# Down-projection weight pairs in the ring of the up projection's weight tiles

## The chip, the cores and the metric

One core of one Trainium2 chip. The metric is the device time of one execution in microseconds; the number told is the median of several runs of the same program. The kernel is written with a tile framework: the program names tiles out of pools ("rings" of a fixed number of buffers under one tag), and a scheduler sets the order of the instructions on each engine when the program is built, then adds the waits. An engine takes its instructions in that order. A tile can be written only when the last user of the buffer that it gets is done.

## The reference

A decoder of two layers on one sequence of 1024 tokens, model width 1024. Each layer:

```
h   = x @ W_in                     # columns split among four mixers
y_A = multi-head latent attention  # causal softmax, rotary keys
y_B = Mamba-2 SSD                  # causal convolution on x/B/C, chunked scan
y_C = multi-scale retention        # rotary q/k, chunkwise recurrence
y_D = RG-LRU branch                # causal convolution, gates, linear recurrence
x   = LayerNorm(alpha * x + concat(y_A, y_B, y_C, y_D) @ W_out)
x   = LayerNorm(alpha * x + SwiGLU(x))   # hidden width 2816
```

## The kernel before

All matrix products run on TensorE in tiles of 128 x 128 weights against 512 columns. Each float32 operand is split into a rounded part and a remainder, and a product is three matmuls: high by high, high by low, low by high. The rounded part is a copy on ScalarE (`A`, ACT), the remainder a subtraction on VectorE (`V`, DVE; L127 is the line of the helper `tt`, so most of the two-operand operations of DVE and of GpSimd, `G`, POOL, stand under L127).

The feed-forward part uses a seven-product scheme of Strassen's kind for 2 x 2 blocks, in both of its projections. In the up projection the hidden width is cut into NF = 22 tiles f. Tiles 0 and 1 are done plainly (`f_plain`), while `x_sums` makes the sums of the input blocks on VectorE and GpSimd. Then `f_block(f)` runs for f = 2 to 21. It loads two rows of weights (`g`, `u`, tiles named `raw`, 512 KB each), casts and splits `g` (`gw`) and half of `u` (`uw`), makes four sums in place on GpSimd (L127, raw<-raw), splits the two results (`s12`, `s34`; with `gw` the tiles named `ws`), and runs seven products of 12 matmuls, 84 in all. The hidden halves go to DRAM (`ha_d`), with sums of them by `to_h`: for each pair of tiles GpSimd makes one difference `s3` and three more, deferred in `later`.

The down projection needs sums of its own weights. They are made inside the same loop by `w2_sums(j)`, for NP = 11 pairs of rows: two loads (w2s<-in_w_f, L1098, L1099), four operations on GpSimd in place (w2s<-w2s), and two write-backs to DRAM (wt_d<-w2s, L1105, L1106). After the loop the down projection goes through seven products m, four token groups t, 11 row pairs j: `b_load(m, j)` loads half a row (`w2r`), casts it and subtracts (tile `w2`), `a_load` the hidden tiles, `behind` adds the product to the accumulators, and a layer norm ends the rows of m = 5 and 6.

Where the tiles live matters for this case. Pool tag "T" has 14 buffers of 128 x 1024 float32; from it come, among others, the inputs of the attention (`ks` and the like), the outputs of the convolutions (`cv`, L628 to L631), the tables of the rotary embedding (`posi`, `posf`, `ang`: `rope_table`, L309, called for tables 1 and 2 in layer 0 by `ret_tables`), the sums of the inputs `xs`, the tiles `w2s`, and most tiles `w2` of the down projection. Tag "raw" has two buffers, and serves the loads of all projection weights (`load_w`, L199, and L410) and of `f_block`.

The DMA issues of the program stand almost all in SP's queue (`nc.sync`), and in its order: a load that waits for its buffer holds back the issues behind it.

Of the kernel before, what the change touches and what calls it, by code (L numbers as in the profile page):

```python
# [9 lines left out]
F32 = mybir.dt.float32  # L10
F32R = mybir.dt.float32r
# [10 lines left out]
NF = DFF // 128  # L22
NP = NF // 2
# [69 lines left out]
def trunk(ctx, tc, xT, xtok, pos, w_in, w_kd, w_att, w_lru, w_out, w_f1, w_f2, par, ln, con, out, dbg=None, depth=DEPTH, stop=None):  # L93
# [5 lines left out]
    wp = ctx.enter_context(tc.tile_pool(name="wp", bufs=1))  # L99
    tp = ctx.enter_context(tc.tile_pool(name="tp", bufs=1))  # L100
# [2 lines left out]
    dp = ctx.enter_context(tc.tile_pool(name="dp", bufs=1, space=bass.MemoryType.DRAM))  # L103

    def T(name, dt=F32):
        return tp.tile([128, 1024], dt, name=name, tag="T", bufs=14)

    def Pt(name, dt=F32):
        return tp.tile([128, 1024], dt, name=name, tag="P", bufs=4)
# [1 line left out]
    def H(name, dt=F32):  # L111
        return tp.tile([128, 512], dt, name=name, tag="H", bufs=11)
# [13 lines left out]
    def tt(out, a, b, op, eng=V):  # L126
        eng.tensor_tensor(out=out, in0=a, in1=b, op=op)  # L127
# [10 lines left out]
    def act(out, a, f, **k):  # L138
        A.activation(out=out, in_=a, func=f, **k)  # L139
# [12 lines left out]
    def mm(out, l, r, start, stop, more=False):  # L152

        PE.matmul(out=out, lhsT=l, rhs=r, start=start, stop=stop, **({"skip_group_check": True} if more else {}))  # L154
# [29 lines left out]
    def sub_f32(out, raw, hi, eng=V):  # L184
        tt(out, raw, hi.bitcast(F32), ALU.subtract, eng)
# [7 lines left out]
    def wpair(name, kind=None):  # L193
        if kind is None:
            kind = kinds.pop(0)
            kinds.append(kind)
        return [wtile(name, part, kind) for part in "hl"]

    def load_w(src, eng=V, kind=None, between=None):  # L199
        raw = wp.tile([128, 1024], F32, name="raw", tag="raw", bufs=2)  # L200
        hi, lo = wpair("w", kind)
        for c in (slice(0, 256), slice(256, 1024)) if between else (slice(0, 1024),):
            nc.sync.dma_start(out=raw[:, c], in_=src[:, c])
            A.copy(out=hi[:, c], in_=raw[:, c])  # L204
            sub_f32(lo[:, c], raw[:, c], hi[:, c], V if c.stop == 256 else eng)
            if between and c.stop == 256:
                between()
        return hi, lo
# [79 lines left out]
    def run(*lists):  # L288
        for l in lists:
            for f in l:  # L290
                f()
# [53 lines left out]
    for L in range(depth):  # L345
# [61 lines left out]
            act(ckr[:, c], ps, AF.Identity, scale=row(pr, P_GKV))  # L407
        run(in_steps("ckv", ev)[:2])

        wr = wp.tile([128, 1024], F32, name="raw", tag="raw", bufs=2)  # L410
        nc.sync.dma_start(out=wr[:, 0:512], in_=w_kd[L])
        wkd = wtile("wkd", "h", "w").rearrange("p (k m) -> p k m", k=KT)
        wr = wr[:, 0:512].rearrange("p (k m) -> p k m", k=KT)
# [29 lines left out]


        wah, wal = load_w(w_att[L], kind="w")
        wqh, wql = (w[:, 0:512].rearrange("p (k m) -> p k m", k=2) for w in (wah, wal))
        wkh, wkl = wah[:, 512:1024], wal[:, 512:1024]
# [617 lines left out]
        def to_h(f, hf, src):  # L1065
# [26 lines left out]
                put(S4, s4)  # L1092
            later.append(rest)

        def w2_sums(j):

            r0, r1 = T("w2s"), T("w2s")
            nc.sync.dma_start(out=r0, in_=w_f2[L, 2 * j])  # L1098
            nc.sync.dma_start(out=r1, in_=w_f2[L, 2 * j + 1])  # L1099
            b11, b12, b21, b22 = (r[:, c] for r in (r0, r1) for c in HALF)  # L1100
            tt(b11, b12, b11, ALU.subtract, G)
            tt(b12, b22, b12, ALU.subtract, G)
            tt(b22, b22, b11, ALU.subtract, G)
            tt(b21, b21, b22, ALU.subtract, G)
            nc.sync.dma_start(out=wt_d[2 * j], in_=r0)  # L1105
            nc.sync.dma_start(out=wt_d[2 * j + 1], in_=r1)  # L1106
# [48 lines left out]

        def f_block(f):

            g, u = (wp.tile([128, 1024], F32, name="raw", tag="raw", bufs=2) for _ in range(2))
            nc.sync.dma_start(out=g, in_=w_f1[L, 2 * f])
            nc.sync.dma_start(out=u, in_=w_f1[L, 2 * f + 1])  # L1160
            gw, s12, s34 = (wpair("ws") for _ in range(3))
            uw = [H("uw", F32R), H("uw", F32R)]

            def split(w, r):
                A.copy(out=w[0], in_=r)  # L1165
                sub_f32(w[1], r, w[0])
            split(gw, g)
            split(uw, u[:, HI])

            tt(g[:, LO], g[:, LO], u[:, LO], ALU.subtract, G)  # L1170
            tt(u[:, LO], u[:, LO], u[:, HI], ALU.add, G)
            tt(u[:, HI], u[:, HI], g[:, LO], ALU.subtract, G)
            split(s12, u)
            tt(g[:, HI], g[:, HI], u[:, HI], ALU.subtract, G)
            split(s34, g)

            run(later)
            later.clear()
            if f % 2 == 0 or f == NF - 1:
                w2_sums(f // 2 - 1 if f < NF - 1 else NP - 1)  # L1180

            def prod(bank, w, c, x_):
                ps = bank()
                wh, wl = (v.rearrange("p (k m) -> p k m", m=128)[:, 4 * c:4 * c + 4] for v in w)
                for k in range(4):
                    if isinstance(x_, int):
                        bh, bl = sums[x_][k]
                    else:
                        bh, bl = (v[:, 4 * x_[0] + k, HALF[x_[1]]] for v in (xh, xl))
                    mm(ps, wh[:, k], bh, k == 0, False)  # L1190
                    mm(ps, wh[:, k], bl, False, False)
                    mm(ps, wl[:, k], bh, False, k == 3)
                return ps

            p, q, r, s = (H("fb") for _ in range(4))
            A.copy(out=p, in_=prod(bankA, gw, 0, (0, 0)))
            tt(q, p, prod(bankB, s12, 1, 1), ALU.add)
            tt(r, q, prod(bankB, s34, 0, 2), ALU.add)
            tt(s, r, prod(bankB, uw, 0, 3), ALU.add)
            ps = prod(bankB, s12, 0, 0)  # L1200
            tt(r, r, ps, ALU.add)
            tt(q, q, ps, ALU.add)
            tt(p, p, prod(bankA, gw, 1, (1, 0)), ALU.add)
            act(p, p, AF.Silu)
            tt(p, p, s, ALU.mult)
            to_h(f, 0, p)
            tt(q, q, prod(bankA, s34, 1, (1, 1)), ALU.add)
            act(q, q, AF.Silu)
            tt(q, q, r, ALU.mult)
            to_h(f, 1, q)  # L1210
# [10 lines left out]
        for f in range(2, NF):  # L1221
            f_block(f)
# [8 lines left out]
        w2 = w_f2[L]  # L1231
# [5 lines left out]
        def b_load(m, j):  # L1237

            st_ = H("w2r")
            nc.sync.dma_start(out=st_, in_=prods[m][1](j))  # L1240
            t_ = (Pt if j in (3, 7) else T)("w2", F32R)
            A.copy(out=t_[:, LO], in_=st_)
            sub_f32(t_[:, HI], st_, t_[:, LO])
            return t_
# [41 lines left out]
        fresh = [lambda t: bankO() if t < 2 else bankA(), lambda t: bankB()]  # L1286
        a_next = a_load(0, 0)
        bs, nbs = [b_load(0, j) for j in range(NP)], []
        gb = None
        for m in range(7):  # L1290
# [110 lines left out]
```

## Time and profile before

| | |
|---|---|
| Median of 3 runs | 2451.14 us (2447.89 to 2457.19) |
| Profiled execution | 2450.49 us; span of the trace 2448.7 us |
| TensorE (PE) busy | 2350.9 us, 96% |
| VectorE (DVE) busy | 1550.6 us, 63% |
| ScalarE (ACT) busy | 930.8 us, 38% |
| GpSimd (POOL) busy | 874.5 us, 36% |
| Mean granted TensorE clock | 0.981 of 2.4 GHz |
| HBM | 222.57 MB read, 81.86 MB written |

The profile is of one execution. "Busy" sums the time in which an engine executed something; a share is an average over stages that have different limits. A row of a group gives its count, busy time, mean time of one, and the idle time of the engine just before, with what ended it (the releaser). The table by stretches gives the same engine totals for pieces of the span, with the granted clock (PEclk; 1.00 is 2.4 GHz, and the lower level is 1.2 GHz) and the mean share of the DMA engines. Layer 0 takes about the first half of the span; its loop over f = 2 to 21 begins at 615.55 us, that of layer 1 at 1824.00 us.

### The profile page before, as it was taken

How to read it: one execution, taken by the hardware profiler on the slowest of the kernel's cores; microseconds unless marked ns; L12 is line 12 of the kernel's file. 1: busy time of each engine (PE TensorE's matmuls, PEld its weight loads, DVE VectorE, ACT ScalarE, POOL GpSimd, SP SyncE). 2: the span in 40 equal slices, each digit the busy share in tenths (PEclk: the TensorE clock that was granted, in tenths of full speed). 3: DMA queues.
4: the chain of work that ended last, by engine and by line, in shares of the span. 5: the costliest groups of instructions: out<-in, count | busy, mean ns of one | idle time of the engine just before them, and what ended most of it. 6: DMA issues, size and time to landing. Idle time of an engine off the chain costs nothing.

```text
span 2448.7 us, 30288 instructions
## 1 busy us (share of the span) xinstructions
PE 2350.9 (96%) x11128; PEld 1882.7 (77%) x11128; DVE 1550.6 (63%) x2445; ACT 930.8 (38%) x1527; POOL 874.5 (36%) x578
## 2 busy tenths in 40 slices
PE   8998999998889999999999999999979899999998
PEld 6776777887667888888887777778767678888886
DVE  6867575579655555665848557655885555557557
ACT  4656344333222232444435553433322222225442
POOL 2440332036876443200323404110377763441003
PEclk9998999999999999999999999999999999999999
DMA  5011211422676333866420103114226663339663
GB/s 181 18 44 61 79 57 52 129 78 78 214 226 212 104 108 100 302 224 193 159 69 26 52 18 95 39 52 156 99 68 215 216 192 109 112 103 329 198 184 123
DMA packets 185764, 310.61 MB, mean 127 GB/s; under 512 B 15104, under 2 KB 101392, under 8 KB 185616
## 3 DMA queue, kind: packets, MB, share of 16 engines
q1 hardware_dynamic: 174048, 280.37, 36.3%
q10 hardware_dynamic: 11568, 28.32, 3.5%
q8 instruction: 87, 1.43, 0.2%
q14 instruction: 61, 0.50, 0.1%
HBM read 222.57 MB, written 81.86 MB: 124 GB/s over the span
## 4 chain that ended last, share of the span: by engine, by line
PE 54%; DVE 5%; POOL 4%; DMA 3%; issue 2%; ACT 1%; DVEq 0%; POOLq 0%; SPq 0%; ACTq 0%
PE pa L154 24%; PE pb L154 23%; PE po L154 6%; DMA raw<-in_w_f 2%; POOL raw L127 1%; POOL w2s L127 1%; DVE acc L127 1%; PE po L562 1%; DVE ws L127 1%; DVE xd L127 1%; ACT ws L1165 0%; DMA wt_d<-w2s 0%; DVE xl L127 0%; POOL acc L127 0%; ACT acc L139 0%
## 5 line engine op out<-in xcount | busy, mean ns | idle before, releaser
L154 PE MATMUL pa<-xh,w 128*128 128x512 f32 x1600 | 526.0, 404 | 12.0 <-ACT xh L342 6.6
L154 PE MATMUL pb<-xs,ws 128*128 128x512 f32 x1440 | 365.6, 402 | 54.1 <-ACT ws L1165 45.6
L154 PEld LDWEIGHTS pb<-xs,ws 128*128 128x128 f32 x1440 | 275.8, 194 | 126.1 <-ACT ws L1165 53.2
L154 PEld LDWEIGHTS pa<-xh,w 128*128 128x128 f32 x1600 | 303.0, 192 | 79.7 <-ACT xh L342 7.4
L154 PE MATMUL pa<-xl,w 128*128 128x512 f32 x800 | 323.9, 405 | 1.1 <-DVE xl L127 1.1
L127 POOL TENSOR_TENSOR raw<-raw 128x512 f32<-128x512 f32 x160 | 221.3, 1383 | 263.6 <-DMA raw<-in_w_f 140.9
L154 PE MATMUL pa<-xh,ws 128*128 128x512 f32 x960 | 308.6, 390 | 0.0
L1165 ACT CAST ws<-raw 128x1024 fp32r<-128x1024 f32 x120 | 126.2, 1051 | 444.0 <-POOL raw L127 333.7
L127 POOL TENSOR_TENSOR w<-raw,w 128x1024 fp32r<-128x1024 f32 (+1 forms) x46 | 117.1, 2545 | 379.5 <-ACT w L204 273.1
L127 DVE TENSOR_TENSOR ws<-raw,ws 128x1024 fp32r<-128x1024 f32 x120 | 158.6, 1322 | 145.0 <-ACT ws L1165 145.0
L127 DVE TENSOR_TENSOR fb<-fb,pb 128x512 f32<-128x512 f32 x200 | 133.6, 684 | 179.2 <-PE pb L154 133.7
L214 POOL TENSOR_TENSOR lrs<-rst,mhalf 128x1 f32<-128x1 f32 x32 | 22.1, 691 | 572.4 <-DVE rst L133 568.4
L154 PE MATMUL po<-w,xh 128*128 128x512 f32 x672 | 211.2, 391 | 0.0
L154 PEld LDWEIGHTS pa<-xh,ws 128*128 128x128 f32 x960 | 180.7, 188 | 37.7 <-DVE fb L127 0.2
L154 PE MATMUL pb<-w,xh 128*128 128x512 f32 x656 | 203.9, 389 | 0.0
L154 PE MATMUL pa<-xl,ws 128*128 128x512 f32 x480 | 187.0, 390 | 0.0
L154 PEld LDWEIGHTS pa<-xl,w 128*128 128x128 f32 x800 | 153.5, 192 | 34.8 <-DVE xl L127 2.5
L127 DVE TENSOR_TENSOR xl<-xl,xh 128x512 fp32r<-128x512 f32 (+1 forms) x168 | 112.1, 679 | 100.0 <-ACT xh L1258 99.4
L1258 ACT CAST xh<-xl 128x512 fp32r<-128x512 f32 (+1 forms) x168 | 97.6, 585 | 201.9 <-DMA xl<-ha_d 190.1
L154 PEld LDWEIGHTS po<-w,xh 128*128 128x128 f32 x672 | 126.3, 188 | 25.8
L127 POOL TENSOR_TENSOR w2s<-w2s 128x512 f32<-128x512 f32 x88 | 126.5, 1437 | 54.3 <-DMA w2s<-in_w_f 47.9
L154 PEld LDWEIGHTS pb<-w,xh 128*128 128x128 f32 x656 | 123.2, 188 | 25.5
(320 smaller groups left out, 4270.7 us busy)
## 6 DMA issues: line engine op xcount, KB each, us to landing
raw<-in_w_f SPq DMA_DIRECT2D x88, 512.0 KB, 4.2
ha_d<-fb SPq DMA_DIRECT2D x120, 256.0 KB, 4.2
xl<-ha_d SPq DMA_DIRECT2D x112, 256.0 KB, 3.6
raw<-in_w_in SPq DMA_DIRECT2D x45, 512.0 KB, 3.6
w2s<-in_w_f SPq DMA_DIRECT2D x44, 512.0 KB, 4.4
wt_d<-w2s SPq DMA_DIRECT2D x44, 512.0 KB, 3.7
w2r<-wt_d SPq DMA_DIRECT2D x88, 256.0 KB, 5.0
w2r<-in_w_f SPq DMA_DIRECT2D x66, 256.0 KB, 5.1
```

The source lines that it names most:

```text
L127: eng.tensor_tensor(out=out, in0=a, in1=b, op=op)
L154: PE.matmul(out=out, lhsT=l, rhs=r, start=start, stop=stop, **({"skip_group_check": True} if more else {}))
L214: G.tensor_tensor(out=out, in0=t, in1=mhalf[:, :n], op=ALU.pow)
L562: PE.transpose(out=ps[:, 128 * b:128 * b + 128], in_=pb[:, 128 * b:128 * b + 128], identity=ident)
L1165: A.copy(out=w[0], in_=r)
L1258: A.copy(out=hi, in_=lo.bitcast(F32))
```

## The change

Pool "T" is cut to 12 buffers and ring "raw" is grown to four, so that the memory used is the same. The tiles `w2s` come from ring "raw". A pair of rows is taken at the eleven tiles f of a list `W2_AT`, about every one and a half tiles, instead of at each even f from 2 on and at f = 21. The condition of `b_load` names the same j (3 and 7) as before, since j is below 11. Lines after 1095 move down by three or less.

```diff
@@ -103,7 +103,7 @@
     def T(name, dt=F32):
-        return tp.tile([128, 1024], dt, name=name, tag="T", bufs=14)
+        return tp.tile([128, 1024], dt, name=name, tag="T", bufs=12)
...
@@ -197,7 +197,7 @@
     def load_w(src, eng=V, kind=None, between=None):
-        raw = wp.tile([128, 1024], F32, name="raw", tag="raw", bufs=2)
+        raw = wp.tile([128, 1024], F32, name="raw", tag="raw", bufs=4)
...
@@ -407,7 +407,7 @@
-        wr = wp.tile([128, 1024], F32, name="raw", tag="raw", bufs=2)
+        wr = wp.tile([128, 1024], F32, name="raw", tag="raw", bufs=4)
...
@@ -1092,9 +1092,12 @@
+        W2_AT = (4, 6, 7, 9, 10, 12, 13, 15, 16, 18, 19)
+
         def w2_sums(j):
 
-            r0, r1 = T("w2s"), T("w2s")
+            r0, r1 = (wp.tile([128, 1024], F32, name="w2s", tag="raw", bufs=4) for _ in range(2))
             nc.sync.dma_start(out=r0, in_=w_f2[L, 2 * j])
             nc.sync.dma_start(out=r1, in_=w_f2[L, 2 * j + 1])
...
@@ -1155,7 +1158,7 @@
         def f_block(f):
 
-            g, u = (wp.tile([128, 1024], F32, name="raw", tag="raw", bufs=2) for _ in range(2))
+            g, u = (wp.tile([128, 1024], F32, name="raw", tag="raw", bufs=4) for _ in range(2))
...
@@ -1176,8 +1179,8 @@
             run(later)
             later.clear()
-            if f % 2 == 0 or f == NF - 1:
-                w2_sums(f // 2 - 1 if f < NF - 1 else NP - 1)
+            if f in W2_AT:
+                w2_sums(W2_AT.index(f))
...
@@ -1238,7 +1241,7 @@
         def b_load(m, j):
...
-            t_ = (Pt if j in (3, 7) else T)("w2", F32R)
+            t_ = (Pt if j % 4 == 3 else T)("w2", F32R)
```

The scheduler orders the program anew. Three places show what moves; the numbers behind names tell the buffers of one name apart.

GpSimd at the beginning of the loop over f in layer 0, before (`xd` and `s3` belong to `x_sums` and `to_h`, `raw_4926` and `raw_4927` to f = 2, the `w2s` to the first pair):

```order
L127 TENSOR_TENSOR xd_4829<-xd_4829,xh_81 128x512
L127 TENSOR_TENSOR s3_4950<-fg_4657,fg_4711 128x512
L127 TENSOR_TENSOR w2s_4959<-w2s_4959 128x512
L127 TENSOR_TENSOR raw_4927<-raw_4927,raw_4926 128x512
L127 TENSOR_TENSOR xd_4851<-xd_4851,xh_81 128x512
L127 TENSOR_TENSOR fg_4711<-fg_4711,fg_4922 128x512
L127 TENSOR_TENSOR w2s_4959<-w2s_4960,w2s_4959 128x512
L127 TENSOR_TENSOR raw_4926<-raw_4926,raw_4927 128x512
L127 TENSOR_TENSOR fg_4657<-fg_4711,fg_4657 128x512
L127 TENSOR_TENSOR w2s_4960<-w2s_4960,w2s_4959 128x512
```

and with the change:

```order
L127 TENSOR_TENSOR xd_4829<-xd_4829,xh_81 128x512
L127 TENSOR_TENSOR s3_4950<-fg_4657,fg_4711 128x512
L127 TENSOR_TENSOR raw_4927<-raw_4927,raw_4926 128x512
L127 TENSOR_TENSOR xd_4851<-xd_4851,xh_81 128x512
L127 TENSOR_TENSOR fg_4711<-fg_4711,fg_4922 128x512
L127 TENSOR_TENSOR raw_4926<-raw_4926,raw_4927 128x512
L127 TENSOR_TENSOR fg_4657<-fg_4711,fg_4657 128x512
L127 TENSOR_TENSOR fg_4824<-fg_4824,fg_4657 128x512
```

The operations of the first pair, which stood between those of f = 2, are gone from here. With the change the first pair stands at f = 4 (`raw_5203`, `raw_5204`):

```order
L127 TENSOR_TENSOR raw_5203<-raw_5203,raw_5204 128x512
L127 TENSOR_TENSOR s3_5091<-fb_4959,fb_4960 128x512
L127 TENSOR_TENSOR raw_5204<-raw_5204 128x512
L127 TENSOR_TENSOR w2s_5233<-w2s_5233 128x512
L127 TENSOR_TENSOR w2s_5233<-w2s_5234,w2s_5233 128x512
L127 TENSOR_TENSOR w2s_5234<-w2s_5234,w2s_5233 128x512
L127 TENSOR_TENSOR w2s_5234<-w2s_5234 128x512
L127 TENSOR_TENSOR raw_5204<-raw_5204,raw_5203 128x512
L127 TENSOR_TENSOR raw_5203<-raw_5203,raw_5204 128x512
L127 TENSOR_TENSOR raw_5351<-raw_5351,raw_5352 128x512
```

Its four operations stand together, ahead of the last two of f = 4.

SP's queue in layer 0, before (`raw_5077`, `raw_5078` are the tiles of f = 3, `raw_5213` one of f = 4):

```order
L1105 DMA wt_d_87<-w2s_4959 128x1024
L1159 DMA raw_5077<-in_w_f1 128x1024
L1067 DMA ha_d_86<-fg_4657 128x4x128
L1098 DMA w2s_5243<-in_w_f2 128x1024
L1160 DMA raw_5078<-in_w_f1 128x1024
L1067 DMA ha_d_86<-fg_4824 128x4x128
L1106 DMA wt_d_87<-w2s_4960 128x1024
L1099 DMA w2s_5244<-in_w_f2 128x1024
L1105 DMA wt_d_87<-w2s_5243 128x1024
L1067 DMA ha_d_86<-fb_4969 128x4x128
L1098 DMA w2s_5527<-in_w_f2 128x1024
L1159 DMA raw_5213<-in_w_f1 128x1024
```

and with the change (`raw_5203`, `raw_5204` of f = 4, `raw_5351`, `raw_5352` of f = 5, `raw_5487` of f = 6):

```order
L1162 DMA raw_5203<-in_w_f1 128x1024
L1067 DMA ha_d_86<-fg_4657 128x4x128
L1163 DMA raw_5204<-in_w_f1 128x1024
L1067 DMA ha_d_86<-fg_4824 128x4x128
L1067 DMA ha_d_86<-fb_4959 128x4x128
L1101 DMA w2s_5233<-in_w_f2 128x1024
L1102 DMA w2s_5234<-in_w_f2 128x1024
L1067 DMA ha_d_86<-s3_5091 128x4x128
L1108 DMA wt_d_87<-w2s_5233 128x1024
L1162 DMA raw_5351<-in_w_f1 128x1024
L1109 DMA wt_d_87<-w2s_5234 128x1024
L1067 DMA ha_d_86<-fb_5094 128x4x128
L1163 DMA raw_5352<-in_w_f1 128x1024
L1162 DMA raw_5487<-in_w_f1 128x1024
```

Before, a load of the next pair stood behind each write-back, so that three pairs are under way by f = 4. With the change the loads of f = 2 and 3 stand ahead of all this, and the two loads of f = 5 stand behind the write-backs of the first pair, whose buffers they get.

VectorE in the attention of layer 0, before (`mx`, `bias`, `rs` are the softmax's, unit by unit; `posf`, `ang`, `kk` the tables'):

```order
L133 TENSOR_SCALAR ang_2152<-ang_2152,cst_75 128x1024
L552 RECIPROCAL rs_1277<-sm_1259 128x1
L312 CAST posf_2167<-posi_2166 128x1024
L131 TENSOR_SCALAR ang_2152<-ang_2152 128x1024
L131 TENSOR_SCALAR pb_1272<-pb_1272,rs_1277 128x512
L131 TENSOR_SCALAR pb_1274<-pb_1274,rs_1277 128x512
L131 TENSOR_SCALAR ang_2170<-posf_2167,cst_75 128x1024
L538 TENSOR_REDUCE mx_1412<-pb_1414 128x1
L538 TENSOR_REDUCE mx_1436<-pb_1438 128x1
L552 RECIPROCAL rs_1336<-sm_1326 128x1
L133 TENSOR_SCALAR kk_2171<-ang_2170,cst_75 128x1024
```

and with the change, where the first table operation stands:

```order
L131 TENSOR_SCALAR pb_1805<-pb_1805,rs_1808 128x384
L538 TENSOR_REDUCE mx_1908<-pb_1910 128x1
L312 CAST posf_2149<-posi_2148 128x1024
L538 TENSOR_REDUCE mx_1908<-pb_1914 128x1
L131 TENSOR_SCALAR ang_2152<-posf_2149,cst_75 128x1024
L127 TENSOR_TENSOR mx_1908<-mx_1908 128x1
L133 TENSOR_SCALAR kk_2153<-ang_2152,cst_75 128x1024
L127 TENSOR_TENSOR bias_1920<-mx_1908,nscq_419 128x1
L127 TENSOR_TENSOR sm_1845<-sm_1845 128x1
```

`mx_1908` is of the second last of the 32 units of the attention; `mx_1412` of the 19th. The tables' operations now stand in the last two units and behind them.

## Rows read from the trace of the kernel before

**Rows 1.** The page: engine totals, and two costly groups with the idle time before them.
```profile
PE 2350.9 (96%) x11128; PEld 1882.7 (77%) x11128; DVE 1550.6 (63%) x2445; ACT 930.8 (38%) x1527; POOL 874.5 (36%) x578
...
L154 PE MATMUL pb<-xs,ws 128*128 128x512 f32 x1440 | 365.6, 402 | 54.1 <-ACT ws L1165 45.6
...
L127 POOL TENSOR_TENSOR w2s<-w2s 128x512 f32<-128x512 f32 x88 | 126.5, 1437 | 54.3 <-DMA w2s<-in_w_f 47.9
```

**Rows 2.** Stretches of the feed-forward loop: busy us (instructions) of each engine.
```profile
core 0: us, PE busy (x) PEld busy (x) DVE busy (x) ACT busy (x) POOL busy (x), PEclk, DMA share, GB/s
600.00:620.00 20.00, 8.73 (x30) 6.27 (x30) 18.30 (x14) 6.63 (x11) 18.90 (x12) 0.75 0.13 39
620.00:780.00 160.00, 145.12 (x609) 114.60 (x608) 92.79 (x98) 41.42 (x54) 124.03 (x86) 0.98 0.72 232
780.00:980.00 200.00, 200.00 (x884) 165.75 (x883) 108.23 (x140) 58.01 (x76) 83.27 (x65) 1.00 0.38 106
1830.00:2004.00 174.00, 157.88 (x652) 125.73 (x653) 94.41 (x106) 44.08 (x57) 125.67 (x89) 0.96 0.69 217
```

**Rows 3.** Timeline, 604 to 618 us: start, duration, instruction, [idle before, releaser].
```profile
611.04 1.71 POOL L127 TENSOR_TENSOR w2s<-w2s 128x512 f32<-128x512 f32 x1
...
612.71 1.71 POOL L127 TENSOR_TENSOR raw<-raw 128x512 f32<-128x512 f32 x1
...
615.55 1.22 PE L154 MATMUL pb<-xs,ws 128*128 128x512 f32 x2 [10.81 <-ACT ws L1165]
```

**Rows 4.** Groups of TensorE's instructions from 620 to 780 us.
```profile
L154 PE MATMUL pb<-xs,ws 128*128 128x512 f32 x273 | 72.1, 409 | 14.9 <-ACT ws L1165 10.9 <-DVE ws L127 4.0
```

**Rows 5.** One tile, w2s: its operations (ns min/median/max), waits and landing times.
```profile
L127 POOL TENSOR_TENSOR w2s<-w2s x88: 1262/1292/2311, 611.0 to 1995.9; 128x512 f32<-128x512 f32 x88
...
  DMA w2s<-in_w_f: 47.9, 26
...
DMA to landing us min/median/max: 2.6/3.9/7.2
```

**Rows 6.** Chain of waits from 1880 to 1910 us, in order of time.
```profile
1887.03 3.91 DMA wt_d<-w2s
...
1890.95 5.71 DMA w2s<-in_w_f
```

**Rows 7.** One tile, raw, from 800 to 1000 us.
```profile
L127 POOL TENSOR_TENSOR raw<-raw x42: 1277/1290/1615, 800.9 to 991.6; 128x512 f32<-128x512 f32 x42
L1165 ACT CAST ws<-raw x32: 1048/1054/1062, 802.2 to 994.2; 128x1024 fp32r<-128x1024 f32 x32
L127 DVE TENSOR_TENSOR ws<-raw,ws x32: 1214/1225/1339, 803.3 to 995.3; 128x1024 fp32r<-128x1024 f32 x32
```

**Rows 8.** DMA issues from 620 to 780 us: count, KB each, median us to landing.
```profile
wt_d<-w2s SPq DMA_DIRECT2D x21, 512.0 KB, 3.4
w2s<-in_w_f SPq DMA_DIRECT2D x20, 512.0 KB, 4.0
raw<-in_w_f SPq DMA_DIRECT2D x16, 512.0 KB, 4.5
```

**Rows 9.** Table by stretches, attention and what follows, columns as in rows 2.
```profile
200.00:240.00 40.00, 33.89 (x206) 21.55 (x204) 27.34 (x81) 26.97 (x65) 1.81 (x1) 0.83 0.20 66
1420.00:1440.00 20.00, 19.76 (x137) 12.71 (x137) 13.56 (x50) 13.68 (x39) 0.00 (x0) 1.00 0.10 27
...
240.00:300.00 60.00, 58.64 (x386) 47.13 (x383) 31.13 (x73) 23.38 (x51) 17.38 (x10) 1.00 0.24 71
```

**Rows 10.** Groups of VectorE's instructions from 184 to 260 us.
```profile
L136 DVE SCALAR_TENSOR_TENSOR ang<-kk,ang 128x1024 f32<-128x1024 f32 x6 | 7.3, 1218 | 0.1
```

**Rows 11.** One tile, cv: the shifted products of the convolution.
```profile
L136 DVE SCALAR_TENSOR_TENSOR cv<-r_B,hp,cv x12: 1259/1277/3410, 122.8 to 1356.6; 128x1023 f32<-128x1023 f32 x4, 128x1022 f32<-128x1022 f32 x4, 128x1021 f32<-128x1021 f32 x4
```

**Rows 12.** Table by stretches, down projection, columns as in rows 2.
```profile
1046.00:1084.00 38.00, 38.00 (x169) 31.47 (x169) 24.35 (x41) 17.24 (x32) 0.00 (x0) 1.00 0.73 252
1180.00:1220.00 40.00, 40.00 (x194) 33.33 (x193) 37.12 (x61) 18.78 (x30) 18.34 (x15) 1.00 0.45 143
```

## The prediction

> **What bounds the kernel now.** I read the page first. TensorE is busy for 2350.9 of the 2448.7 us of the span [rows 1], so nothing but its idle time, and the time in which it runs at the lower clock, can be won here. The next view is the table by stretches, to see where that time lies. In the feed-forward part of layer 0 from 780 to 980 us TensorE is busy for 200.00 of 200 us, with 884 matmuls, at full clock [rows 2]: 0.226 us per matmul, so 19.0 us for one weight tile of 84 matmuls. In the first 160 us of the same loop (620 to 780) it is busy for 145.12 us, at a mean clock of 0.98, and does 609 matmuls, where 160 us at the later pace would hold 707: 22.2 us are lost. In layer 1 from 1830 to 2004 us it does 652 where 769 would fit: 26.5 us. Together 48.7 us, which is 2.2 us for each of the 22 pairs of down-projection rows. Ahead of the stretch lies one long gap of 10.81 us [rows 3], and the 20 us around it ran at a mean clock of 0.75 [rows 2]; layer 1 has the like.
>
> What does TensorE wait for there? By the groups of that stretch it is the ScalarE cast and the VectorE subtraction that make `ws` (10.9 and 4.0 us) [rows 4], and the casts wait for GpSimd. GpSimd is busy 78% of the stretch before 780 us (124.03 of 160) and 42% after (83.27 of 200) [rows 2]. The difference is the w2s work: 88 operations of 1.44 us on average [rows 1], which run from 611.0 to 1995.9 us, in the first eight tiles or so of each layer's loop; 47.9 us of GpSimd's own idle time goes to their loads [rows 5]. GpSimd works in order: while the head of its row waits for a w2s load, the operations on `raw` behind it stand still, and `ws`, and TensorE. The chain of waits shows it: a write-back of 3.91 us, then the load that takes its place, 5.71 us [rows 6], and so on, pair after pair. Each load of a pair waits there for the tile of the one before.
>
> **The change part by part.**
>
> *The pairs are spread out.* The 11 calls move from f = 2, 4, 6 ... (which the built order runs ahead, one after another) to f = 4, 6, 7, 9 ... 19, and their tiles stand in the ring of `raw`. A pair can no longer be loaded before the tile whose slots it takes is split, so the order cannot bunch them. Work is neither added nor removed: 88 GpSimd operations, 44 loads and 44 stores remain. GpSimd then has for three tiles and two pairs 12 operations on `raw` of 1.29 us [rows 7], 8 on w2s of 1.44 us, and six for the hidden sums at about the same 1.4 us: 15.5 + 11.5 + 8.4 = 35.4 of 57.1 us. That is 62%, between the 78% at which TensorE stalls and the 42% at which it does not.
>
> The longest chain in the new order is: two w2s loads go out when the slots of an earlier tile are split, four sums, the write-backs, the next tile's `raw` loads into the same slots, its four operations, cast, subtraction. With rows: load 4.0 + 4 x 1.44 + store 3.4 + load 4.5 + 4 x 1.29 + cast 1.05 + subtraction 1.23 [rows 1, 5, 7, 8] = 25.1 us; with the slower load and store of the chain (5.71 and 3.91 [rows 6]) 27 us; and with up to three hidden sums that may come between (4.3 us) about 31 us. Two tiles of TensorE are 38.1 us. The chain fits, with 7 us to spare, less where two pairs stand at neighbouring tiles (f = 6 and 7, 9 and 10 ...). So the full price of the stretch is 48.7 us if nothing stalls; the lower bound is nothing, if each pair stalls as before. I take 38 us, because the first tiles (f = 2 and 3) still wait for loads and GpSimd after the gap, and f = 4, the first tile with a pair, has little ahead of it.
>
> *The gap before the loop.* In the old order a w2s operation of 1.71 us stands at 611.04 us just before the `raw` operation that ends the gap (612.71, then the cast, then TensorE at 615.55) [rows 3]. The new order has none there. That is 1.7 us per layer, and a little less of the lower clock: 3 us for both.
>
> *A load on SP waits longer.* SP issues in order, and the load of the next tile now waits for a write-back; behind it stand the stores of hidden halves, whose tiles come free later. In the old order the loads of a pair waited for write-backs in the same way. I cost it at nothing: what covers it is the same 7 us of the chain.
>
> *Two general tiles fewer.* Pool T has 12 tiles instead of 14 for everything else, in both layers. Three places used more than 12 at once, and the built order moves there.
>
> (a) The rope tables of layer 0 used free tiles inside the attention: their VectorE work stood between the softmax operations from 185 to 220 us. From 200 to 240 us TensorE is busy for 33.89 of 40 us at a clock of 0.83, that is 6.1 us idle and 0.17 x 40 = 6.8 us of clock; layer 1 makes no tables, and the like stretch from 1420 is busy for 19.76 of 20 us at full clock [rows 9]. So the tables cost up to 12.9 us there. In the new order they begin two units of attention before its end and go on after it. What hides them there: VectorE is busy for only 31.13 of 60 us from 240 to 300 [rows 9], and the tables are some 20 us (22 whole-tile operations, of which the six costliest are 7.3 us [rows 10], the others 0.7 to 1.3 us each). If they delay the state-space part that follows, part comes back. Bounds: 12.9 us won and 5 us lost; I take 6 won.
>
> (b) Two of the convolutions come some 20 us later in each layer, three VectorE operations of 1.27 us each (3.41 at worst [rows 11]) amid the second half of the attention. In layer 1 VectorE is busy for 13.56 of 20 us from 1420 to 1440 [rows 9], at the end of that half, so they fit. Bounds 0 and 3 us; I take 1.5.
>
> (c) In the down projection the weights of j = 4 and 5 are cast later, just before use. VectorE is busy for 24.35 of 38 us from 1046 to 1084 [rows 12], so 14 us are free for some 8 us of late work; where layer norms fall together with it, from 1180 to 1220, VectorE is already at 37.12 of 40 us, and TensorE had no gap. Bounds 0 and 4 us; I take 1.5.
>
> **Sum.** -38 - 3 - 6 + 1.5 + 1.5 = -44 us, against the profiled execution of 2450.49 us: 2406 us. The median of the runs is 2451.14, 0.65 us above, which I leave out.
>
> **A rule against it.** GpSimd is slower where VectorE is full: from 600 to 620 us, with VectorE busy for 18.30 of 20 us [rows 2], its operations take 1.71 us one after the other [rows 3]; after 800 us, with VectorE at 54%, 1.29 us is the median on `raw` [rows 7]; the extremes on w2s are 1.26 and 2.31 us [rows 5]. The Trainium skill, SBUF — State Buffer, section "SBUF: two separate sides", gives a reason: operations of VectorE with two inputs in SBUF and those of GpSimd share a pair of ports, which one of them holds for its whole instruction while the other is blocked. The rows agree. By that rule each moved sum may block VectorE, and be blocked, at tiles that were free of it; by the rows after 800 us the sums above stand, and -44 with them. What it does at its worst is case 4 below, worked out from the 2.31 us.
>
> **The rivals.**
>
> 1. *As above.* 2406 us, own range 2392 to 2416. For it: 200.00 of 200 us wherever GpSimd has no w2s work, and the sums by rows. Chance 0.56.
>
> 2. *The loss is only halved.* Each pair still stalls TensorE for 1.1 us, since its four sums stand ahead of the last two `raw` operations of a tile and wait for a load: 24 of the 48.7 us are won. With the other terms as above (-3 - 6 + 3 = -6): 2450.5 - 24 - 6 = 2420 us. Chance 0.22.
>
> 3. *The stalls move with the pairs.* 2.2 us per pair as before, only spread from f = 4 to 19, and the moved tables cost elsewhere what they gave. What is left is 3 us, and 2 to 3 for the tail of attention: 2445 us. For it: in the old order too the chain was write-back, load, sums, and a ring of four is shorter than what the pairs had. Against it: 22 pairs then fell on 16 tiles, now on 32. Chance 0.12.
>
> 4. *The ring becomes the bound, and it is slower.* The place is the load of the tile after a pair. Eight GpSimd operations at the 2.3 us of [rows 5], not 1.29 to 1.44, make the chain 31 + 7.5 = 38.5 us, no longer under the 38.1 of two tiles; with the first load at 7.2 us, the longest [rows 5], and the second at the 5.71 of [rows 6], it is 41.2. TensorE then stops 3.1 us for each pair: 22 x 3.1 = 68, in place of 48.7; with the -6 us elsewhere this gives 2464 us. It decides from a stall of 2.2 us per pair on. Against it: the subtractions of `ws` after 800 us stay at 1.23 us and `raw` operations at 1.29 at the median [rows 7], although TensorE runs there without a gap, so VectorE's load leaves them room. Chance 0.10.
>
> That the change moves nothing is excluded by the built order.
>
> **How the numbers follow.** The predicted time is that of case 1. The range takes in cases 1 to 3 but for their tails: 2392 to 2446 us; it leaves out case 4 (0.10) and some 0.10 below and above. A measurement of this kernel tells about 0.5% (12 us) from no change, that is 2439 to 2463. Faster: cases 1 and 2, 0.78. Within it: case 3, 0.12. Slower: case 4, 0.10.
>
> **What would show it.** Right: from 620 to 780 us TensorE is busy for over 155 us at full clock and GpSimd for about 62%; w2s operations run until some 960 us; the wait ahead of `pb<-xs,ws` falls from 54.1 us [rows 1] to under 30; from 200 to 240 us TensorE has less than 3 us idle. Wrong: gaps of 1 to 3 us in each tile with a pair, ended by the cast of `ws` after a GpSimd operation on `raw` that waited for its load (cases 2 to 4); VectorE operations beside w2s at 2 us and more (case 4); new gaps at 260 to 340 us, by the tables, or in the down projection, by late weights.

## The result, and the profile after

The changed kernel takes 2390.89 us (median of 4 runs, 2390.16 to 2392.41) against 2449.51 us (2447.31 to 2457.19) for the kernel before: a ratio of 0.9757, with a 95% interval of 0.974 to 0.9773. That is 58.6 us less. The forecast was 2406 us, 44 us less, with a range from 2392: the sign and the place were right, the gain was more than forecast by a third, and the time is 1.1 us below the range. The profiled execution took 2390.16 us, 1.8 us more than its span.

The page of the changed kernel, its header, engine totals and the groups that answer to [rows 1]:

```profile
span 2388.4 us, 30277 instructions
...
PE 2324.8 (97%) x11128; PEld 1869.7 (78%) x11128; DVE 1585.0 (66%) x2445; ACT 927.9 (39%) x1525; POOL 882.1 (37%) x578
...
L154 PE MATMUL pb<-xs,ws 128*128 128x512 f32 x1440 | 352.4, 393 | 23.2 <-ACT ws L1168 18.9
...
L127 POOL TENSOR_TENSOR raw<-raw 128x512 f32<-128x512 f32 x160 | 237.9, 1487 | 225.9 <-DVE uw L127 106.5
...
L127 POOL TENSOR_TENSOR w2s<-w2s 128x512 f32<-128x512 f32 x88 | 120.1, 1365 | 36.1 <-DMA w2s<-in_w_f 25.9
```

The idle time ahead of `pb<-xs,ws` has fallen from 54.1 to 23.2 us. What is left lies at the beginning of each loop: one gap of 9.4 us, and a second one of 2.13 us behind it (TensorE's timeline, layer 0 and then layer 1):

```profile
602.78 1.22 PE L154 MATMUL pb<-xs,ws 128*128 128x512 f32 x2 [9.35 <-ACT ws L1168]
606.13 4.34 PE L154 MATMUL pb<-xs,ws 128*128 128x512 f32 x12 [2.13 <-DVE ws L127]
...
1786.39 1.22 PE L154 MATMUL pb<-xs,ws 128*128 128x512 f32 x2 [9.37 <-ACT ws L1168]
1789.75 4.71 PE L154 MATMUL pb<-xs,ws 128*128 128x512 f32 x12 [2.13 <-DVE ws L127]
```

The table by stretches shows the loop, and the end of the attention of layer 0:

```profile
core 0: us, PE busy (x) PEld busy (x) DVE busy (x) ACT busy (x) POOL busy (x), PEclk, DMA share, GB/s
200.00:240.00 40.00, 39.45 (x283) 26.46 (x280) 31.92 (x98) 26.68 (x75) 4.15 (x2) 1.00 0.14 40
...
600.00:620.00 20.00, 15.09 (x57) 11.88 (x58) 14.39 (x14) 4.80 (x6) 13.34 (x9) 0.78 0.40 119
620.00:780.00 160.00, 159.95 (x706) 132.10 (x706) 102.95 (x114) 47.81 (x63) 104.42 (x75) 1.00 0.58 176
780.00:980.00 200.00, 200.00 (x884) 165.62 (x883) 119.35 (x141) 58.46 (x79) 112.28 (x81) 1.00 0.61 185
...
1800.00:1976.00 176.00, 175.80 (x775) 145.04 (x774) 113.51 (x126) 52.47 (x68) 110.41 (x79) 1.00 0.57 174
```

From 620 to 780 us TensorE now does 706 matmuls, where [rows 2] had 609, and is idle for 0.05 us; in layer 1 it does 775 in 176 us, where [rows 2] had 652 in 174. GpSimd is busy 65% in the first of these stretches and 56% from 780 to 980: the work that filled one stretch is in both. The DMA engines went from a share of 0.72 and 0.38 to 0.58 and 0.61. The attention's stretch from 200 to 240 us has 39.45 us of TensorE at full clock, where [rows 9] had 33.89 at 0.83.

The chain of waits in the loop, which [rows 6] had running through write-backs and loads, is now TensorE's own:

```profile
by line: PE pb L154 58.5%; PE pa L154 37.7%; DMA raw<-in_w_f 5.1%; ACT ws L1168 3.7%; issue 0.1%; ACTq L1168 0.0%
22 pieces in order of time: start us, us, what
635.96 4.10 DMA raw<-in_w_f
...
640.15 2.96 ACT ws L1168 x3
...
643.16 10.73 PE pb L154 x46
653.89 5.44 PE pa L154 x24
```

(From 640 to 720 us; behind the last row only TensorE follows.)

To see where the time came from, I took the start of the same numbered matmul in both traces; both do 11128, in nearly the same stages. The table gives the time of each stage before, and by how much other kernels differ from it there (us; the kernels other than the changed one come below; "before again" is a second execution of the kernel before).

| Matmuls | Stage | Before | Changed | t12 | ring_even | ring_dense | notab_before | notab_after | w2raw | before again |
|---|---|---|---|---|---|---|---|---|---|---|
| 0 to 1200 | layer 0 to the end of attention | 250.9 | -11.6 | -12.0 | -12.0 | -11.5 | -13.7 | -12.7 | -11.7 | +2.1 |
| to 2951 | other mixers, output, plain tiles | 348.6 | +0.3 | +2.5 | +6.5 | +1.3 | -0.5 | -3.2 | -0.2 | 0.0 |
| to 2952 | gap before the loop | 11.2 | -1.5 | -1.4 | -1.4 | -1.4 | 0.0 | -1.4 | -1.4 | 0.0 |
| to 4000 | loop over f, first part | 262.5 | -20.3 | -20.2 | -18.9 | -15.9 | -1.2 | -18.6 | -19.0 | -1.3 |
| to 5400 | loop's rest, down projection | 316.4 | 0.0 | +50.6 | 0.0 | 0.0 | 0.0 | 0.0 | 0.0 | 0.0 |
| to 5600 | layer norms at its end | 41.3 | +2.2 | +2.5 | +3.6 | +2.2 | -0.1 | +3.7 | +2.1 | +0.3 |
| to 8547 | layer 1 ahead of its gap | 577.0 | -5.4 | -1.9 | +3.0 | -5.3 | -4.7 | -4.9 | -3.3 | +0.1 |
| to 8548 | gap | 11.2 | -1.4 | -1.4 | -1.4 | -1.4 | 0.0 | -1.4 | -1.4 | 0.0 |
| to 9600 | loop, first part | 268.1 | -24.2 | -24.4 | -23.4 | -17.6 | -3.2 | -24.5 | -24.4 | -3.1 |
| to 11127 | rest | 346.1 | 0.0 | +48.5 | 0.0 | 0.0 | 0.0 | 0.0 | 0.0 | 0.0 |

The stages of the changed kernel sum to -61.9; its end, from the last matmul to the end of the span, is 1.5 us longer (11.6 against 10.1 us), so the span is 60.3 us shorter.

### The profile page after: what moved, and what is told of

The parts are those of the page before. It is cut to its first block, busy times and chain, and to the rows that moved or that the text cites. A ratio compares the mean times of both kernels' runs of the same rounds, so it can differ in the third digit from the quotient of the medians.

```text
span 2388.4 us, 30277 instructions
## 1 busy us (share of the span) xinstructions
PE 2324.8 (97%) x11128; PEld 1869.7 (78%) x11128; DVE 1585.0 (66%) x2445; ACT 927.9 (39%) x1525; POOL 882.1 (37%) x578
## 4 chain that ended last, share of the span: by engine, by line
PE 80%; DVE 11%; issue 2%; ACT 2%; DMA 2%; POOL 1%; ACTq 0%; DVEq 0%; SPq 0%; POOLq 0%
PE pa L154 37%; PE pb L154 34%; PE po L154 8%; DVE acc L127 2%; PE po L562 1%; DVE xs L127 1%; DVE xl L127 1%; DVE xd L127 1%; DVE acc L136 1%; ACT acc L139 1%; POOL acc L127 1%; DVE bst L991 1%; DVE w L127 1%; DVE ws L127 1%; DVE seg L127 1%
## 5 line engine op out<-in xcount | busy, mean ns | idle before, releaser
L154 PE MATMUL pb<-xs,ws 128*128 128x512 f32 x1440 | 352.4, 393 | 23.2 <-ACT ws L1168 18.9
L127 POOL TENSOR_TENSOR raw<-raw 128x512 f32<-128x512 f32 x160 | 237.9, 1487 | 225.9 <-DVE uw L127 106.5
L214 POOL TENSOR_TENSOR lrs<-rst,mhalf 128x1 f32<-128x1 f32 x32 | 22.1, 689 | 555.9 <-DVE rst L133 555.9
L127 DVE TENSOR_TENSOR ws<-raw,ws 128x1024 fp32r<-128x1024 f32 x120 | 163.9, 1390 | 13.2 <-ACT ws L1168 13.0
L127 POOL TENSOR_TENSOR w2s<-w2s 128x512 f32<-128x512 f32 x88 | 120.1, 1365 | 36.1 <-DMA w2s<-in_w_f 25.9
```

The costliest lines, as they stand in the source:

```text
L214: G.tensor_tensor(out=out, in0=t, in1=mhalf[:, :n], op=ALU.pow)
```

## The experiments

The theory: in the kernel before, the pairs' GpSimd operations, loads and write-backs, bunched in the first eight tiles, starved the loop; the ring of four spreads them. The cut of pool T drives the rope tables out of the attention. Rivals: it is the deeper ring, or the list of places, that fills the loop; and something else than the tables stalled the attention.

**Pool T alone (t12).**

```
 def T(name, dt=F32):
-    return tp.tile([128, 1024], dt, name=name, tag="T", bufs=14)
+    return tp.tile([128, 1024], dt, name=name, tag="T", bufs=12)
```

> The kernel before with pool T cut to 12 tiles and nothing else (ring raw stays at two, the pairs stay in T at the even f). In the built order no pair finds a free T tile during the loop: all 11 pairs of a layer now stand behind f = 21. Theory (the moved pairs are what stalled the loop, and the cut of T is what frees the attention): up to the first loop it is 11 to 13 us earlier than the kernel before, as the changed kernel is; both loops run at 19.0 us per tile, so 20 and 25 us less; what then comes is the pairs' work at the start of the down projection, 44 GpSimd operations of 1.3 us = 57 us per layer, partly covered by the first two products (some 60 us): 0 to 30 us lost per layer. Total 2392 to 2450 us. Rival (the ring of four raw tiles, by loading deeper, is what fills the loop): the loops keep gaps of more than 8 us per layer, although no pair is in them. Rival for the attention (the deeper ring, not T): the attention keeps its gaps at 200 to 240 us. For layer 1 ahead of its loop, where the changed kernel won 5.5 us that were not forecast: if the moved buffers did it, it is there here too; if it is how the lower clock happened to fall, it may be there or not.

Measured: 2494.56 us in one run, 43.6 us more than the median of before beside it. The attention gained 12.0 us, as in the changed kernel, with the ring still at two: the cut of T does it. (T at 12 has less room for everything, so it is not a lack of tiles that had stalled the attention.) The loop, with no pair in it, gained 20.2 and 24.4 us, again as the changed kernel did (20.3 and 24.2). So the deeper ring isn't needed to fill the loop, and the changed kernel won all that the pairs had cost there, to within 0.2 us. The rows of this kernel by stretches (columns as above): the loop, and then the beginning of the down projection:

```profile
611.80:771.80 160.00, 160.00 (x707) 132.47 (x707) 87.88 (x115) 46.86 (x61) 69.24 (x53) 1.00 0.39 110
...
980.00:1040.00 60.00, 18.69 (x71) 14.88 (x71) 19.85 (x20) 10.04 (x17) 53.77 (x39) 0.63 1.04 413
```

and its longest wait of TensorE (total, times, longest):

```profile
PE po L154 <- ACT w L1242: 41.3, 1, 41.3
```

The bill comes behind the loop: 50.6 and 48.5 us, where I had expected 0 to 30 per layer. From 980 to 1040 us GpSimd is busy for 53.77 of 60 us and the DMA engines are full (share 1.04, 413 GB/s), and TensorE waits 41.3 us in one piece for the cast of a weight tile. Work taken out of the loop altogether costs more than it did in it; it must go into the loop, but thinly.

**The ring with the old places (ring_even).**

```
-            if f in W2_AT:
-                w2_sums(W2_AT.index(f))
+            if f % 2 == 0 or f == NF - 1:
+                w2_sums(f // 2 - 1 if f < NF - 1 else NP - 1)
```

> The changed kernel with the pairs called at the old places (f = 2, 4, 6 ... 20, 21), still in the ring of four. Theory (the ring spreads the pairs, since a pair can't load before an earlier tile is split; the list of places is secondary): the loop runs at 19.0 us per tile but for its first two tiles, where the first pair now meets the gap: 1 to 4 us per layer more than the changed kernel, 2392 to 2400 us. Rival (the list is what counts, the ring bunches as pool T did): the loop loses some 15 to 25 us per layer as before, 2425 us and more.

Measured: 2408.11 us (2 runs), ratio to the kernel before 0.9826 (0.9763 to 0.989), and 17 us more than the changed kernel, between both expectations. The loops agree with the theory: -18.9 and -23.4 us, within 1.4 us of the changed kernel in each. So the ring spreads the pairs without the list. (The list without the ring was not run. The program with the list, but with the pairs in pool T at 14 tiles, is built in the same order on every engine as the kernel before, so the list moves nothing by itself.) What the old places cost lies ahead of the loops, where neither expectation had it: 6.2 us more in layer 0 and 8.4 in layer 1 than in the changed kernel. The pair of f = 2 now comes at the beginning of the plain tiles, while the layer norm ahead of them is still under way. In layer 0 its four sums on GpSimd run from 550.26 to 558.57 us. The small operation `lrs` of that layer norm (L214) stands behind the first of them and a `raw` operation, VectorE waits for it, and TensorE then has a gap ahead of the transposes of the result (L1015). GpSimd's timeline, then TensorE's:

```profile
550.26 1.55 POOL L127 TENSOR_TENSOR w2s<-w2s 128x512 f32<-128x512 f32 x1 [1.11 <-DMA w2s<-in_w_f]
551.76 1.71 POOL L127 TENSOR_TENSOR raw<-raw 128x512 f32<-128x512 f32 x1
553.44 0.54 POOL L214 TENSOR_TENSOR lrs<-rst,mhalf 128x1 f32<-128x1 f32 x1
...
555.86 0.63 PE L1015 MATMUL pb<-cst,acc 128*128 128x128 f32 x4 [3.67 <-issue]
```

Behind the gap come 6.8 us at the lower clock (from 556.5 us), which the changed kernel doesn't have; layer 1 has the same at 1751 us, with a gap of 3.48 us. It is this that the list's late start at f = 4 saves.

**A pair in each tile (ring_dense).**

```
-        W2_AT = (4, 6, 7, 9, 10, 12, 13, 15, 16, 18, 19)
+        W2_AT = (4, 5, 6, 7, 8, 9, 10, 11, 12, 13, 14)
```

> The changed kernel with a pair at each tile from f = 4 to f = 14. This tests the price of the chain. Theory as predicted (load of the pair, sums, write-back, the next tile's load into its buffers, its operations, cast and subtraction, 25 us or more, and two tiles' time of 38 us to do it in): with a pair in each tile the chain has only one tile of 19.0 us, so tiles f = 4 to 14 take 25 us or more: some 6 us lost for each of 22 pairs, 130 us, 2500 to 2530 us; clearly slower. Rival (the two rows of a pair and the two of a tile overlap, so that the chain never binds): no loss, 2391 us within 5. In between (1 to 3 us for each pair): the chain binds, with a shorter length than worked out, 2410 to 2460 us. GpSimd alone needs about 13.4 of 19.0 us per tile and does not bind.

Measured: 2402.68 us in one run, 11.8 more than the changed kernel. The loops lost 4.4 and 6.6 us against it, 11 us for 22 pairs: 0.5 us for each, not 6. The rival is nearer. The timeline of this kernel shows why my period was wrong:

```profile
701.71 0.34 SPq L1101 DMA_DIRECT2D w2s<-in_w_f  x1
703.40 0.33 SPq L1102 DMA_DIRECT2D w2s<-in_w_f  x1
706.11 1.29 POOL L127 TENSOR_TENSOR w2s<-w2s 128x512 f32<-128x512 f32 x1 [5.54 <-DMA w2s<-in_w_f]
...
714.61 0.33 SPq L1162 DMA_DIRECT2D raw<-in_w_f  x1
...
721.01 0.33 SPq L1101 DMA_DIRECT2D w2s<-in_w_f  x1
```

The load of the next pair goes out at 721.01, 19.3 us after the last, when the `raw` load issued at 714.61 has only just landed (718.2). It takes the buffers of the tile before, whose split on VectorE the load waits for. The ring has two halves, each of which serves a pair and then a tile, so each half has two tiles' time, 38 us, also with a pair in each tile. The chain of 25 to 31 us of the prediction fits into that; the step from there to "one tile's time" in this expectation was the error. It also means that the changed kernel had more slack than I gave it.

**The tables left out of the kernel before, and out of the changed one (notab_before, notab_after).** Both have this edit:

```
         def ret_tables():
-            if L == 0:
-                rope_table(1)
-                rope_table(2)
             for i in (1, 2):
                 t_ = T("cs")
-                nc.scalar.dma_start(out=t_, in_=tab_d[i])
+                nc.scalar.dma_start(out=t_, in_=tab_d[0])
```

> The kernel before without the two rope tables that layer 0 makes for the retention (table 0 is read in their place, so the retention's rotary angles are left out of the computation). Theory (the tables' VectorE work between the softmax operations cost the attention 12.9 us, gaps and lower clock): from 200 to 240 us TensorE is busy for over 39 us at full clock and the attention ends 11 to 13 us earlier; the rest as before; 2436 to 2440 us. Rival (what stalls the tail of the attention in layer 0 is something else that the smaller pool T moved, such as the convolutions): the gaps stay, less than 4 us won.

Measured: 2428.27 us in one run, 22.7 less than the median beside it; more than expected, but the attention is as expected: 13.7 us less, and this row by stretches, for [rows 9]:

```profile
200.00:240.00 40.00, 39.31 (x268) 26.12 (x265) 28.51 (x101) 28.33 (x79) 2.81 (x2) 1.00 0.08 28
```

The tables were the cause, not another tile of pool T. The other 9 us came in stages that the tables have no part in, and in which this kernel is ordered as the kernel before: 4.7 us in layer 1 ahead of its loop, 1.2 and 3.2 in the loops. The loops' part comes in a second execution of the unchanged kernel too (1.3 and 3.1 us, last column of the table), so it is no effect of the edit. More on the rest below.

> The changed kernel without the two tables of the retention in layer 0 (table 0 read in their place, so the rotary angles of the retention are left out of the computation). Against the kernel before the changed one was 11.6 us ahead at the end of the attention and 8.9 us at 400 us; the kernel before without tables stayed 13.4 to 13.9 us ahead. Theory (the tables, now behind the attention, delay the state-space part and the retention): without them the changed kernel is 13 to 14 us ahead both at the end of the attention and at 400 us; 2386 to 2389 us. Rival (what it gives back after the attention is due to the smaller pool, tables or not): still 9 us ahead at 400 us; 2391 us.

Measured: 2389.18 us in one run. At 400 us (matmul 2000) it is 13.5 us ahead of the kernel before, where the changed kernel is 8.9 ahead; at the beginning of the loop 17.4 against 12.8. So the tables, put behind the attention, still cost the changed kernel some 4.6 us of layer 0, where they cost 13.7 in the attention of the kernel before: moving them was worth about 9 us, by one execution of each. That the total is only 1.7 us below the median of the changed kernel (the span 1.0 us below its traced one) comes of differences in later stages: 1.7 us less won in the first loop, 1.5 us lost at the layer norms, and 0.5 us less won in layer 1 ahead of its loop.

**The kernel before once more.**

> The kernel before once more, unchanged. In layer 1 ahead of its loop (from 1236 to 1812 us) the changed kernel won 5.4 us that no term of the prediction held; the kernel without tables, which is ordered there as the kernel before is, won 4.7 us in the same place. Theory (where the lower clock falls there differs from one execution to the next): this execution needs a different time for that stage than the profiled one of before, by 2 to 6 us, with other stretches at half clock, or at least other stretches in some stage by 2 us and more. Rival (the stage takes the same time always, and the buffers moved made the difference): the stage is within 1 us of before, with the same stretches at 1514, 1617 and 1774 us.

Measured: 2448.18 us. The stage in layer 1 that I had in mind took 577 us again, within 0.1; inside it the time differs by 3.4 us on the way (at matmul 8000) and comes back. In the attention this execution lost 2.1 us more, with TensorE's clock lower still; the row by stretches, for [rows 9]:

```profile
200.00:240.00 40.00, 35.12 (x166) 21.22 (x164) 25.30 (x77) 25.62 (x62) 0.43 (x1) 0.69 0.19 66
```

In the first trace 13.7 us of the attention ran at 1.2 GHz, in this one 27.3 us. So the price of a stall in clock does differ between executions of one program by some microseconds, but for the stage in question the two agree. The two loops took 1.3 and 3.1 us less than in the first trace: of the 44.5 us that the changed kernel won there, 40.1 are left against this execution. The kernel notab_before, whose order in layer 1 was not changed by its edit, has the stage 4.7 us shorter. Its trace holds 6.8 us at the lower clock there, the two of the kernel before 17.1 and 20.5, the changed kernel 6.8 (half of the difference to 17.1 is 5.1 us, and the stage is 5.4 us shorter). By that sum most of the 5.4 us are the lower clock. The sum is not exact: the second execution of before had 3.4 us more at the lower clock in the same time, and t12 holds 6.8 us as well and won only 1.9. That the 5.4 us are owed to the change isn't shown, and notab_before speaks against it.

**The tiles of the down projection (w2raw).**

```
-            t_ = (Pt if j % 4 == 3 else T)("w2", F32R)
+            if j in (5, 9):
+                t_ = wp.tile([128, 1024], F32R, name="w2", tag="raw", bufs=4)
+            else:
+                t_ = (Pt if j % 4 == 3 else T)("w2", F32R)
```

> The changed kernel with the weight tiles w2 of j = 5 and 9 in ring raw, which stands idle in the down projection, so that 14 instead of 18 of them share the 12 tiles of pool T. All variants with T at 12 lost 2.2 to 3.6 us between the end of the first down projection's products and the layer norms behind it, and the kernel without tables with T at 14 lost nothing there. Theory (late casts of w2 meet the layer norms on VectorE): this loss of 2.2 us in layer 0 goes, and the end of the program, 1.5 us longer in the changed kernel, shortens by about as much: 2387 to 2389 us. Rival (the loss comes from something else that T held there, such as accumulators or the next layer's tiles): 2391 us within 1.

Measured: 2391.13 us (4 runs), ratio to the kernel before 0.9769 (0.9741 to 0.9798): no difference to the changed kernel. The loss at the layer norms stayed (+2.1 us), so the rival holds there: the late casts of the w2 tiles alone are not its cause. All kernels here with T at 12 have it (2.1 to 3.7 us), those with 14 don't (at most 0.3); which other tile of T it is stays open. The end of the span was 10.1 us after the last matmul, 1.5 less than in the changed kernel, as expected, so there the theory holds; layer 1 ahead of its loop took 2.1 us more, again with more of the lower clock (13.7 us).

**A version that beats both (plain3s).** What is left at the loops of the changed kernel are the gaps before them, 9.4 us, with another of 2.1 us behind each. A third plain tile covers them:

```
         run(p1[1][1:])
-        for f in range(2, NF):
+        run(f_plain(2))
+        for f in range(3, NF):
             f_block(f)
...
-        W2_AT = (4, 6, 7, 9, 10, 12, 13, 15, 16, 18, 19)
+        W2_AT = (5, 7, 8, 10, 11, 13, 14, 16, 17, 19, 20)
```

> The changed kernel with a third plain tile (f = 2) behind the input sums, and the places of the pairs one tile later. It is for what still stops TensorE: the gaps of 9.4 and 2.1 us at the beginning of each loop, while GpSimd and VectorE finish the sums, and the lower clock after them (10.2 and 13.7 us at half speed, so 5 to 7 us). A plain tile has 96 matmuls where a block has 84: 12 x 0.226 = 2.7 us more per layer. Theory (the gap is only the sums being late by about 10 us, and 21.7 us of plain work cover them): both gaps and most of the clock's cost go, 15 to 18 us per layer less the 2.7: 2391 - 25 to 30 = 2361 to 2366 us. Rival (GpSimd and VectorE are so loaded there that the first block, with its own four operations, is late all the same): half of it or less, 2375 us and more.

Measured: 2368.71 us (4 runs, 2368.09 to 2368.76), ratio to the kernel before 0.9678 (0.9655 to 0.9702), and 22 us less than the changed kernel. The rows by stretches of this kernel, around the place where the gaps were:

```profile
560.00:600.00 40.00, 40.00 (x178) 33.14 (x177) 35.97 (x33) 10.52 (x17) 28.35 (x18) 1.00 0.07 20
600.00:760.00 160.00, 160.00 (x708) 132.45 (x707) 103.56 (x115) 49.02 (x66) 109.09 (x78) 1.00 0.56 173
...
1740.00:1780.00 40.00, 40.00 (x178) 33.12 (x177) 37.35 (x35) 12.46 (x21) 27.06 (x17) 1.00 0.09 27
```

Both gaps and the lower clock behind them are gone, in both layers, for 2 x 12 matmuls more (5.4 us). The time is 2.7 us above the upper end of the expectation; where these went was not followed up.

## Why the prediction was right or wrong

**The place and the mechanism were right.** *The pairs are spread out*: the loop's stalls were the pairs', and they are gone; t12 shows it by a loop without pairs (20.2 and 24.4 us), the changed kernel has the same with them. Case 2 (half of the stalls stay), case 3 (they move along) and case 4 (the ring binds) all fell, since TensorE is idle for 0.05 us from 620 to 780 us and for 0.20 us from 1800 to 1976. Which part of the bunched pairs did the harm, their GpSimd operations, their loads or their write-backs, no run separates; the three moved together.

**The step that failed is the choice between the bounds, in two terms, and a third gain had no term.** The first: "I take 38 us, because the first tiles (f = 2 and 3) still wait ... and f = 4 ... has little ahead of it". The bound from counted matmuls was 48.7 us, and 44.5 came (20.3 + 24.2). Of the first tiles only one gap of 2.1 us is left, and f = 4 has none. The reserve of 10.7 us rested on no row. The chain had 7 us to spare in my own sum, and ring_dense shows that a pair in each tile, instead of two in three tiles, costs only 0.5 us per pair. Of the 6.5 us that this term was short, 4.4 hang on the execution: against the second trace of the kernel before the loops won 40.1 us, so there 38 was short by 2.1.

The second: (a), the tables, "Bounds: 12.9 us won and 5 us lost; I take 6 won". The stretch of [rows 9] gave 12.9; the attention won 11.6, the tables gave some 4.6 back behind it (notab_after), and other differences of the same stage made good for most of that, so that 11.3 us were kept up to the gap before the loop. I had taken a middle of the bounds where the row of layer 1 (19.76 of 20 us busy, no tables) was a measurement of the term. Against the second trace of before layer 0 won 13.4 us up to its gap, so the terms of layer 0 were 6 to 8 us short.

**What no term held**: 5.4 us in layer 1 ahead of its loop, with less time at the lower clock (6.8 against 17.1 us), where the forecast had 0.75 us lost. No run ties it to an instruction that the change moves, and notab_before, whose order there is that of the kernel before, had 4.7 us of it too; the cause stays open. It should have stood in the range: two executions of the kernel before differ by 2.1 us in the attention alone. The range was too narrow by its own terms, too: their favourable bounds add up to 48.7 + 3 + 12.9 = 64.6 us, which is 2386 us, and it stopped at 2392.

**The smaller terms.** *The gap before the loop*: 3 us forecast, 2.9 measured (9.35 instead of 10.81 us in layer 0). *The convolutions*: 1.5 us forecast; in layer 1 from 1236 to 1462 us of the trace of before (matmuls 5600 to 6800) the changed kernel falls back by 0.6 us, so it was less. *The down projection*: 1.5 us forecast, 2.2 measured in layer 0, none in layer 1 but 1.5 at the end of the span; the sign was right, but of the reason given, late casts of w2, w2raw bears out only the 1.5 us at the end.

| Term | Forecast | Measured | Against the second trace of before |
|---|---|---|---|
| loops | -38 | -44.5 | -40.1 |
| gaps before them | -3 | -2.9 | -2.9 |
| layer 0 up to its gap | -6 and +0.75 | -11.3 | -13.4 |
| layer norms, end of the span | +1.5 | +3.7 | +3.9 |
| layer 1 up to its gap | +0.75 | -5.4 | -5.4 |
| sum | -44 | -60.3 | -58.0 |

(The sum of the terms is to the span; by the profiled executions too it is 60.3 us, by the medians 58.6.)

**The rule against it.** The Trainium skill, SBUF — State Buffer, section "SBUF: two separate sides", has a GpSimd operation and a VectorE operation with two inputs in SBUF block each other, and by that the moved sums should lengthen the work of both where they now stand. The trace agrees in the main: `raw` operations take 1487 ns in the mean, against 1383 before, and VectorE is busy for 1585.0 us, against 1550.6 [rows 1], with the same 2445 instructions; its operations `fb<-fb` alone rose from 840 to 1157 ns, 25.5 of the 34.4 us. The pairs' own operations became shorter (1365 ns, against 1437). It did not change the time, since neither engine binds in the loop: GpSimd is at 56 to 65% and VectorE at 60 to 64% from 620 to 980 us.

## What to carry to other kernels

Where a trace has the same loop once stalled and once not, the count of instructions done in each gives the whole price of the stall, lower clock and refilling included (48.7 us here against 31 us of idle time in the same two stretches); if no row shows what would be left of it, take the price nearly whole. Background work that shares an in-order engine with the critical path belongs in the loop at a density that leaves the chain slack: bunched at the front it cost 40 to 44.5 us, taken out to the end 99 us, spread no more than a loop without it (within 0.2 us). A ring shared by two kinds of tile is a cheap way to spread it, since a load can't run ahead of the buffers; a list of places in the program alone moved nothing in the built order here.

## What the runs showed of the hardware

The price of one and the same stall in clock is not fixed: with the same program the attention's tail ran 13.7 us at 1.2 GHz in one execution and 27.3 us in another, 2.1 us apart in the end. The spread of the runs differs as well: measured side by side, seven runs of the kernel before range over 13.6 us (2440.55 to 2454.13), four of w2raw over 2.1 us (2389.8 to 2391.88), and four of plain3s, without the gaps before the loops, over 0.7 us (2368.09 to 2368.76). That the stalls' price in clock makes this spread fits, but no run shows it.
